# A fused multiply and GELU on one core: two DRAM stretches of 64 KB rows, two stores, and x opened by the heads of its rows

## The chip, the cores and the metric

The kernel runs on one core of a Trainium2 chip. The metric is the device time of one execution in microseconds; the figure given is the median of several runs. A profile of one execution shows when each engine worked and when each DMA packet moved.

## The reference

```python
batch, dim = 1024, 4096          # x and y: float32, normally distributed
z = x * y
out = (0.5 * z * (1 + np.tanh(np.sqrt(2 / np.pi) * (z + 0.044715 * z ** 3)))).astype(np.float32)
```

Every element stands by itself. The kernel reads two arrays of 16.78 MB and writes one, 50.33 MB in all.

## The kernel before

Since the operation is elementwise, the kernel treats each array as one flat run of 4,194,304 values and may give any part of it to any of the 128 partitions, as long as x, y and the output agree. On chip, `xs` holds 32,768 values in each partition, all of x at once; the product and the result are written over it in place. `ys` holds 20,440 values in each partition, so y does not fit whole: its later part reuses room that the first part has left.

The flat run is cut into three pieces (`PIECES`), by columns of `xs`: columns 0 to 1280, 1280 to 17664 and 17664 to 32768. In DRAM each piece is one stretch without holes; the helper `columns` gives partition p the p-th run of it. One load of a piece is therefore 128 rows, of 5,120, 65,536 and 60,416 bytes. The rows of a transfer are dealt out to 16 DMA engines, eight to each.

The order of the transfers is written out by hand.

- x's small piece goes out from SP's queue and x's 64 KB rows from ACT's queue; `_hoist` moves both to the front of the program, ahead of the opening barrier.
- SP then waits for the small piece of x, and issues y's piece with 64 KB rows and x's third piece.
- y's third piece goes into room that the first three multiplies free, so SP waits for three of them (`Y_FREE`); y's small piece waits for the fourth. They land in `ys` from 0 and from 15104.
- VectorE (DVE) multiplies in the order of `Y_LOADS`: four steps of 4096 columns of the middle piece, then seven of 2048 and one of 768 of the third, then 1280 of the small one (`STEPS`). Before each piece it waits for x and y to have landed. ScalarE (ACT) waits for each multiply and applies GELU in place.
- SP stores the pieces in the same order (`STORES`), each when its activations are done; the first also waits until y's third piece has landed. At the end SP waits for all stores.

All of SP's transfers, loads and stores, stand in one queue in order of issue; in the profile it is q1, and ACT's queue, with x's 64 KB rows, is q10.

Of the kernel before, what the change touches and what calls it, by code (L numbers as in the profile page):

```python
# [1 line left out]

# [4 lines left out]


F32 = mybir.dt.float32
GELU = mybir.ActivationFunctionType.Gelu_apprx_tanh  # L10

PIECES = [(0, 1280), (1280, 17664), (17664, 32768)]

Y_LOADS = [(1280, 17664, 4056), (17664, 32768, 0), (0, 1280, 15104)]

Y_FREE = [0, 3, 4]

STEPS = [[4096] * 4, [2048] * 7 + [768], [1280]]  # L20
STORES = [(1280, 17664), (17664, 32768), (0, 1280)]
Y_BUF = 20440


def _hoist(nc, issued):

    here = nc.cur_bb.bb.instructions
    first = nc.main_func.blocks[0].instructions
    for ins in issued:
        del here[next(k for k, i in enumerate(here) if i is ins or i.name == ins.name)]  # L30
    engine = issued[0].engine
    at = next(
        k
        for k, i in enumerate(first)
        if i.engine == engine and type(i).__name__ == "InstDrain"
    )
    first[at:at] = issued


@with_exitstack  # L40
def kernel(
    ctx: ExitStack,
    tc: tile.TileContext,
    x: bass.AP,
    y: bass.AP,
    out: bass.AP,
):
    nc = tc.nc
    P = nc.NUM_PARTITIONS

    def columns(t, a, b):

        flat = t.flatten_outer_dims().rearrange("r c -> (r c)")
        pa, pb = next(q for q in PIECES if q[0] <= a and b <= q[1])
        return flat[P * pa : P * pb].rearrange("(p c) -> p c", p=P)[:, a - pa : b - pa]


    tc.close()
    tc.compile()  # L59

    xs = nc.alloc_sbuf_tensor("xs", [P, PIECES[-1][1]], F32).ap()
    ys = nc.alloc_sbuf_tensor("ys", [P, Y_BUF], F32).ap()
    sem_x = [nc.alloc_semaphore(f"sem_x{i}") for i in range(len(PIECES))]
    sem_y = [nc.alloc_semaphore(f"sem_y{i}") for i in range(len(Y_LOADS))]
    sem_mul = nc.alloc_semaphore("sem_mul")
    sem_act = nc.alloc_semaphore("sem_act")
    sem_o = [nc.alloc_semaphore(f"sem_o{i}") for i in range(len(STORES))]

    def load_x(i, engine=nc.sync):
        a, b = PIECES[i]  # L70
        return engine.dma_start(out=xs[:, a:b], in_=columns(x, a, b)).then_inc(sem_x[i], 16)

    def load_y(i):
        a, b, r = Y_LOADS[i]
        return nc.sync.dma_start(
            out=ys[:, r : r + b - a], in_=columns(y, a, b)
        ).then_inc(sem_y[i], 16)

    _hoist(nc, [load_x(0).ins])
    _hoist(nc, [load_x(1, nc.scalar).ins])  # L80
    nc.sync.wait_ge(sem_x[0], 16)
    load_y(0)
    load_x(2)
    for i in range(1, len(Y_LOADS)):
        if Y_FREE[i]:
            nc.sync.wait_ge(sem_mul, Y_FREE[i])
        load_y(i)

    n = 0
    done = {}  # L90
    for i, (a, b, r) in enumerate(Y_LOADS):
        for j, (xa, xb) in enumerate(PIECES):
            if xa <= a < xb:
                nc.vector.wait_ge(sem_x[j], 16)
        nc.vector.wait_ge(sem_y[i], 16)  # L95
        c = a
        for w in STEPS[i]:
            nc.vector.tensor_mul(  # L98
                out=xs[:, c : c + w],
                in0=xs[:, c : c + w],  # L100
                in1=ys[:, r + c - a : r + c - a + w],
            ).then_inc(sem_mul, 1)
            n += 1
            done[c + w] = n
            nc.scalar.wait_ge(sem_mul, n)
            nc.scalar.activation(  # L106
                out=xs[:, c : c + w], in_=xs[:, c : c + w], func=GELU
            ).then_inc(sem_act, 1)
            c += w

    for i, (a, b) in enumerate(STORES):
        if i == 0:
            nc.sync.wait_ge(sem_y[-2], 16)
        nc.sync.wait_ge(sem_act, done[b])
        nc.sync.dma_start(out=columns(out, a, b), in_=xs[:, a:b]).then_inc(sem_o[i], 16)
    for i in range(len(STORES) - 1):
        nc.sync.wait_ge(sem_o[i], 16)
    nums = sorted(s.num for s in [*sem_x, *sem_y, *sem_o[:-1], sem_mul, sem_act])
    assert nums == list(range(nums[0], nums[-1] + 1))
    nc.sync.sem_clear(range(nums[0], nums[-1] + 1))  # L120
    nc.sync.wait_ge(sem_o[-1], 16).then_inc(sem_o[-1], -16)


# [1 line left out]
_INS = ['x', 'y']  # L125
_OUTS = [((1024, 4096), 'float32')]


# [23 lines left out]
```

## Time and profile before

| What | Value |
|---|---|
| Median of 3 runs (lowest, highest) | 119.83 us (119.79, 119.85) |
| Span of the profiled execution, first to last instruction | 118.52 us |
| DVE busy, 13 multiplies | 35.2 us |
| ACT busy, 13 activations and a table load | 31.0 us |
| DMA moved | 50.33 MB, mean 425 GB/s, 1296 packets |
| Landings: x's pieces | 13.55, 30.48, 60.41 us |
| Landings: y's pieces | 42.56, 78.25, 79.82 us |
| Landings: stores | 99.19, 116.98, 118.49 us |

The profiled execution has no time of its own beside its span; the median of the runs is 1.31 us longer than that span, since a run's time takes in what lies before the first and after the last instruction. A line such as L98 is a line of the kernel's file; DVE's multiplies carry L98, ACT's activations L106, y's loads L75, x's loads L71 and the stores L115 in the listing of the profile. "Landing" is the moment when all 16 DMA engines have reported a transfer to its semaphore.

### The profile page before, as it was taken

How to read it: one execution, taken by the hardware profiler on the slowest of the kernel's cores; microseconds unless marked ns; L12 is line 12 of the kernel's file. 1: busy time of each engine (PE TensorE's matmuls, PEld its weight loads, DVE VectorE, ACT ScalarE, POOL GpSimd, SP SyncE). 2: the span in 40 equal slices, each digit the busy share in tenths (PEclk: the TensorE clock that was granted, in tenths of full speed). 3: DMA queues.
4: the chain of work that ended last, by engine and by line, in shares of the span. 5: the costliest groups of instructions: out<-in, count | busy, mean ns of one | idle time of the engine just before them, and what ended most of it. 6: DMA issues, size and time to landing. Idle time of an engine off the chain costs nothing.

```text
span 118.5 us, 82 instructions
## 1 busy us (share of the span) xinstructions
DVE 35.2 (30%) x13; ACT 31.0 (26%) x14; POOL 0.2 (0%) x4
## 2 busy tenths in 40 slices
DVE  0000000000000069999920000059999940000000
ACT  4000000000000000977975000006998990000000
POOL 0000000000000000000000000000000000000000
DMA  9888899889988897797797797798899887977975
GB/s 492 382 382 382 354 575 487 354 354 398 664 354 354 354 652 326 326 652 326 326 632 347 326 632 347 326 575 354 354 531 531 354 354 326 652 326 326 652 326 221
DMA packets 1296, 50.33 MB, mean 425 GB/s; under 512 B 144, under 2 KB 144, under 8 KB 528
## 3 DMA queue, kind: packets, MB, share of 16 engines
q1 hardware_dynamic: 1152, 41.94, 82.2%
q10 hardware_dynamic: 144, 8.39, 16.5%
HBM read 33.55 MB, written 16.78 MB: 425 GB/s over the span
## 4 chain that ended last, share of the span: by engine, by line
DMA 55%; DVE 24%; ACT 3%; issue 1%; DVEq 0%
DMA ys<-in_y_dram 43%; DVE xs L98 24%; DMA xs<-in_x_dram 11%; ACT xs L106 3%; DVEq L95 0%
## 5 line engine op out<-in xcount | busy, mean ns | idle before, releaser
L98 DVE TENSOR_TENSOR xs<-xs,ys 128x2048 f32<-128x2048 f32 (+3 forms) x13 | 35.2, 2777 | 60.9 <-DMA ys<-in_y_dram 60.9
L106 ACT ACTIVATE xs<-xs 128x2048 f32<-128x2048 f32 (+3 forms) x13 | 29.7, 2301 | 65.1 <-DVE xs L98 65.1
L106 ACT ACT_TABLE_LOAD x1 | 1.3, 1283 | 1.6 <-PEq L59 1.6
L136 POOL MEMSET const-bfloat16-1.0<- 128x1 bf16 x1 | 0.1, 103 | 0.0
L136 POOL MEMSET const-uint8-127<- 128x1 uint8 x1 | 0.1, 102 | 0.0
L136 POOL MEMSET const-float32-0.0<- 128x1 f32 x1 | 0.1, 100 | 0.2 <-issue 0.2
L136 POOL MEMSET const-float32-1.0<- 128x1 f32 x1 | 0.1, 99 | 0.0
## 6 DMA issues: line engine op xcount, KB each, us to landing
xs<-in_x_dram SPq DMA_DIRECT2D x1, 7552.0 KB, 46.5
ys<-in_y_dram SPq DMA_DIRECT2D x1, 7552.0 KB, 22.5
out_dram<-xs SPq DMA_DIRECT2D x1, 7552.0 KB, 20.4
xs<-in_x_dram SPq DMA_DIRECT2D x1, 640.0 KB, 13.6
ys<-in_y_dram SPq DMA_DIRECT2D x1, 640.0 KB, 19.7
out_dram<-xs SPq DMA_DIRECT2D x1, 640.0 KB, 20.8
xs<-in_x_dram ACTq DMA_DIRECT2D x1, 30.4
ys<-in_y_dram SPq DMA_DIRECT2D x1, 29.0
```

Of the source, the lines that this page charges most:

```text
L98: nc.vector.tensor_mul(out=xs[:, c : c + w], in0=xs[:, c : c + w], in1=ys[:, r + c - a : r + c - a + w],).then_inc(sem_mul, 1)
L106: nc.scalar.activation(out=xs[:, c : c + w], in_=xs[:, c : c + w], func=GELU).then_inc(sem_act, 1)
L136: nc = _bacc.Bacc("TRN2", target_bir_lowering=False, num_devices=1)
```

## The change

The flat run is cut into two halves instead of three pieces (`HALVES`), so that partition p owns one run of 65,536 bytes in each half. A transfer that takes part of a half reads that part of each run: its rows then lie 65,536 bytes apart in DRAM.

- x's first half is loaded as two transfers: 5,120-byte heads of its rows from SP (`HEAD`), the remaining 60,416 bytes of each row from ACT. x's second half is one transfer of 64 KB rows.
- y's first half is one transfer of 64 KB rows; its second half is loaded as the first 48 KB of each row, then the last 16 KB, into `ys` from 0 and from 12288. They wait for three and for four multiplies, as the corresponding loads did.
- The multiplies go through the first half in four steps of 4096, then through the second in six steps of 2048 (48 KB rows) and steps of 2048, 1280 and 768 (16 KB rows).
- There are two stores of 64 KB rows instead of three. The first waits for four activations and for the first multiply of y's second half; the second for all 13 activations.

```diff
-PIECES = [(0, 1280), (1280, 17664), (17664, 32768)]
+HALF = 16384
+HALVES = [(0, HALF), (HALF, 2 * HALF)]
 
-Y_LOADS = [(1280, 17664, 4056), (17664, 32768, 0), (0, 1280, 15104)]
+HEAD = 1280
 
-Y_FREE = [0, 3, 4]
-
-STEPS = [[4096] * 4, [2048] * 7 + [768], [1280]]
-STORES = [(1280, 17664), (17664, 32768), (0, 1280)]
+Y_LOADS = [(0, 16384, 4056, 0), (16384, 28672, 0, 3), (28672, 32768, 12288, 4)]
+STEPS = [[4096] * 4, [2048] * 6, [2048, 1280, 768]]
...
-        pa, pb = next(q for q in PIECES if q[0] <= a and b <= q[1])
-        return flat[P * pa : P * pb].rearrange("(p c) -> p c", p=P)[:, a - pa : b - pa]
+        ha, hb = next(h for h in HALVES if h[0] <= a and b <= h[1])
+        return flat[P * ha : P * hb].rearrange("(p c) -> p c", p=P)[:, a - ha : b - ha]
...
-    _hoist(nc, [load_x(0).ins])
-    _hoist(nc, [load_x(1, nc.scalar).ins])
+    _hoist(nc, [load_x(0, HEAD, sem_x[0]).ins])
+    _hoist(nc, [load_x(HEAD, HALF, sem_x[1], nc.scalar).ins])
     nc.sync.wait_ge(sem_x[0], 16)
     load_y(0)
-    load_x(2)
+    load_x(*HALVES[1], sem_x[2])
     for i in range(1, len(Y_LOADS)):
-        if Y_FREE[i]:
-            nc.sync.wait_ge(sem_mul, Y_FREE[i])
+        nc.sync.wait_ge(sem_mul, Y_LOADS[i][3])
         load_y(i)
...
-    for i, (a, b) in enumerate(STORES):
-        if i == 0:
-            nc.sync.wait_ge(sem_y[-2], 16)
-        nc.sync.wait_ge(sem_act, done[b])
+    first = len(STEPS[0])
+    nc.sync.wait_ge(sem_act, first)
+    nc.sync.wait_ge(sem_mul, first + 1)
+    for i, done in enumerate((first, n)):
+        a, b = HALVES[i]
+        nc.sync.wait_ge(sem_act, done)
         nc.sync.dma_start(out=columns(out, a, b), in_=xs[:, a:b]).then_inc(sem_o[i], 16)
...
```

More of the change, by code (lines that the diff above doesn't have):

```diff
@@ L53, in columns @@
         flat = t.flatten_outer_dims().rearrange("r c -> (r c)")
-        pa, pb = next(q for q in PIECES if q[0] <= a and b <= q[1])
-        return flat[P * pa : P * pb].rearrange("(p c) -> p c", p=P)[:, a - pa : b - pa]
+        ha, hb = next(h for h in HALVES if h[0] <= a and b <= h[1])
+        return flat[P * ha : P * hb].rearrange("(p c) -> p c", p=P)[:, a - ha : b - ha]
     tc.close()
     tc.compile()
-    xs = nc.alloc_sbuf_tensor("xs", [P, PIECES[-1][1]], F32).ap()
+    xs = nc.alloc_sbuf_tensor("xs", [P, 2 * HALF], F32).ap()
     ys = nc.alloc_sbuf_tensor("ys", [P, Y_BUF], F32).ap()
-    sem_x = [nc.alloc_semaphore(f"sem_x{i}") for i in range(len(PIECES))]
+    sem_x = [nc.alloc_semaphore(f"sem_x{i}") for i in range(3)]
     sem_y = [nc.alloc_semaphore(f"sem_y{i}") for i in range(len(Y_LOADS))]
@@ L66, with load_x, load_y @@
     sem_act = nc.alloc_semaphore("sem_act")
[L67 to L75, printed above, removed]
+    sem_o = [nc.alloc_semaphore(f"sem_o{i}") for i in range(2)]
+    def load_x(a, b, sem, engine=nc.sync):
+        return engine.dma_start(out=xs[:, a:b], in_=columns(x, a, b)).then_inc(sem, 16)
+    def load_y(i, engine=nc.sync):
+        a, b, r, _ = Y_LOADS[i]
+        return engine.dma_start(
             out=ys[:, r : r + b - a], in_=columns(y, a, b)
         ).then_inc(sem_y[i], 16)
-    _hoist(nc, [load_x(0).ins])
-    _hoist(nc, [load_x(1, nc.scalar).ins])
+    _hoist(nc, [load_x(0, HEAD, sem_x[0]).ins])
+    _hoist(nc, [load_x(HEAD, HALF, sem_x[1], nc.scalar).ins])
     nc.sync.wait_ge(sem_x[0], 16)
     load_y(0)
-    load_x(2)
+    load_x(*HALVES[1], sem_x[2])
     for i in range(1, len(Y_LOADS)):
-        if Y_FREE[i]:
-            nc.sync.wait_ge(sem_mul, Y_FREE[i])
+        nc.sync.wait_ge(sem_mul, Y_LOADS[i][3])
         load_y(i)
     n = 0
[L90 to L94, printed above, removed]
+    for i, (a, b, r, _) in enumerate(Y_LOADS):
+        if i == 0:
+            nc.vector.wait_ge(sem_x[0], 16)
+            nc.vector.wait_ge(sem_x[1], 16)
+        if i == 1:
+            nc.vector.wait_ge(sem_x[2], 16)
         nc.vector.wait_ge(sem_y[i], 16)
@@ L103 @@
             n += 1
-            done[c + w] = n
             nc.scalar.wait_ge(sem_mul, n)
@@ L109 @@
             c += w
-    for i, (a, b) in enumerate(STORES):
-        if i == 0:
-            nc.sync.wait_ge(sem_y[-2], 16)
-        nc.sync.wait_ge(sem_act, done[b])
+    first = len(STEPS[0])
[4 more added lines that the diff above has]
+        nc.sync.wait_ge(sem_act, done)
         nc.sync.dma_start(out=columns(out, a, b), in_=xs[:, a:b]).then_inc(sem_o[i], 16)
-    for i in range(len(STORES) - 1):
-        nc.sync.wait_ge(sem_o[i], 16)
-    nums = sorted(s.num for s in [*sem_x, *sem_y, *sem_o[:-1], sem_mul, sem_act])
+    nc.sync.wait_ge(sem_o[0], 16)
+    nums = sorted(s.num for s in [*sem_x, *sem_y, sem_o[0], sem_mul, sem_act])
     assert nums == list(range(nums[0], nums[-1] + 1))
     nc.sync.sem_clear(range(nums[0], nums[-1] + 1))
-    nc.sync.wait_ge(sem_o[-1], 16).then_inc(sem_o[-1], -16)
+    nc.sync.wait_ge(sem_o[1], 16).then_inc(sem_o[1], -16)
 _INS = ['x', 'y']
```

## The prediction

> **What bounds the kernel now.** I read the page first: its busy shares and its list of DMA queues.
>
> ```profile
> span 118.5 us, 82 instructions
> DVE 35.2 (30%) x13; ACT 31.0 (26%) x14; POOL 0.2 (0%) x4
> ...
> q1 hardware_dynamic: 1152, 41.94, 82.2%
> q10 hardware_dynamic: 144, 8.39, 16.5%
> ```
>
> No engine that computes is busy for a third of the span, but the packets of the two DMA queues (q1 is SP's, q10 is ACT's) fill 82.2 + 16.5 = 98.7% of what 16 DMA engines could do in it. The chain that ended last seems to say otherwise:
>
> ```profile
> 0.00 13.55 DMA xs<-in_x_dram
> 13.57 28.99 DMA ys<-in_y_dram
> 42.66 13.11 DVE xs L98 x3
> 55.78 22.47 DMA ys<-in_y_dram
> 80.56 13.30 DVE xs L98 x6
> 93.88 3.80 ACT xs L106 x3
> ```
>
> It names 24% DVE, because it goes from issue to issue: y's second load is issued at 55.78, when three multiplies have freed its buffer. Whether that issue is late for the DMA engines it does not say. So I read the DMA by stages (columns: stretch, length, three engines' busy time, clock, DMA share, GB/s):
>
> ```profile
> 13.60:42.60 29.00, 0.00 (x0) 0.00 (x0) 0.00 (x0) 1.00 1.00 431
> 42.60:60.40 17.80, 17.43 (x4) 11.13 (x4) 0.00 (x0) 1.00 1.00 434
> 79.80:99.20 19.40, 16.32 (x9) 15.26 (x9) 0.00 (x0) 1.00 0.99 428
> ```
>
> The DMA share is 1 with and without the multiplies: the engines run at about 431 GB/s whatever DVE does. (A packet is booked where it starts, so short or badly cut stretches show more or less.)
>
> Last I took the trace's packet records (start, duration, bytes, queue) one by one and followed, from the last packet backwards, whichever ended 3 ns after it began. That gives the whole life of the DMA engine that ended last, 81 packets without a hole: 24 of each row size and 9 semaphore writes. In ns:
>
> ```
> row bytes   typical duration   step to the next packet
>  5,120        196                 193
> 60,416       2229                2226
> 65,536       2418                2414.5
>      4          9                   6
> last engine: first packet at 1312, last ends at 118123
> stretched packets: the first two of x (399, 342), the first two on ACT's queue (2549, 2620)
> ```
>
> The sum: 24 x 193 + 24 x 2226 + 24 x 2414.5 + 9 x 6 = 116.06 us. With the start at 1.31 and the stretched packets' excess (203 + 146 + 131 + 202 ns = 0.68) it is 118.05, against 118.12 measured; 0.07 is spread over small stretches. The final write lands 0.37 later, at 118.49, and the span closes at 118.52. The median of the runs, 119.83, lies 1.31 above that span, which I carry over. So what can move the time is: row counts, the first 13 us, a hole in the stream, and the last landing.
>
> **The change part by part.**
>
> *Rows.* Nine transfers of 8 rows per DMA engine become eight, with the same bytes. The steps above lie on a line (2033 ns for the 55,296 bytes between the two smaller sizes, 193 at 5,120), which puts a 49,152-byte row at 1812 and a 16,384-byte row at 607 ns. After, per engine: x's heads 8 x 193 = 1.54; the rest of x's first half 8 x 2226 = 17.81; y's first half, x's second half and two stores 32 x 2414.5 = 77.26; y's second half 8 x 1812 + 8 x 607 = 19.35; semaphores 8 x 6 = 0.05. Sum 116.02: a gain of 0.04 us, all on the path. No large gain is left in fewer rows: a row costs only about 5 ns beyond its bytes.
>
> *Row pitch.* The second half of x and of y and the second store, before in rows packed at 60,416 bytes, go to a 65,536-byte pitch in DRAM. Row of the trace: y's first load has that pitch now and takes 2418 to 2425 a packet, the 60,416-byte rows 2229 to 2246; both are 27.1 bytes per ns. Stores: the first (65,536) averages 2 to 18 ns over 2418 a packet after its first round, the second (60,416) 1 to 18 over 2229. I take nothing, with -0.05 to +0.1 for 8 store rows. The Trainium skill, "DMA: Bandwidth & Descriptors", section "Latency and other measured facts", speaks against such a layout: it has copies slow at row pitches of large powers of two, 207 GB/s at 512 KiB against 214 unimpaired (each DMA engine's eight rows here span that much). By that rule, as an estimate, 7 of 214 (3.3%) of the 25.2 MB that get this pitch, 58 us at 431 GB/s, would be 1.9 us; y's first load shows none of it.
>
> *Start.* x's heads were one packed 640 KB; now each lies at the front of its own 65,536-byte stretch. No row of the trace reads such heads, so bounds. The mean durations of x's five first rounds are 444, 222, 206, 203 and 198: only the first reads are slow. The last engine lost 0.68 in this stage; all of that gone would be -0.68. If instead each of its six later heads were stretched by as much as its second one is (146 ns), it would be +0.88. I take 0: the nearest row, ACT's load at the new pitch with its first packets 126 (mean), then 21 and 1 ns over 2418, says that scattered rows cost once and not on each row.
>
> *Issues, in SP's order; each only matters if the queue runs dry.* An issue brings its first packet about 0.84 later (the first store: 78.27 to 79.11); at the very start 1.01. y's first load waits for x's heads to land: now 13.55, and four ACT packets per engine that lie between the heads shorten by 188 each, so about 12.8. Meanwhile ACT's queue still has four of its eight packets per engine, 8.9 us of cover. x's second half is issued right behind it. y's 48 KB rows wait for multiply 3: y's first half lands 8 x 0.188 = 1.5 earlier (41.05), so the issue comes at 54.27; x's second half feeds the first engine until 59.5 as before, cover 4.4 after the 0.84. y's 16 KB rows wait for multiply 4 at 58.6 and are needed at 74.0.
>
> The first store has a new wait, the first multiply of y's second half. Behind it on SP stand only the second store and the closing waits. The 48 KB rows land at 78.25 - 8 x (2226 - 1812) ns = 74.94, the multiply ends 0.1 + 2.29 later at 77.33, so the first store packet can start at 78.19. The 16 KB rows hold the first engine until 78.89 and the last until 79.38: a cover of 0.70 and more. Today the cover is negative for the first engines (rows end at 78.90, store starts at 79.11; 0.10 us of hole on average: last semaphore writes end at 79.09, store packets start at 79.19 in the mean), while the last engine has none. Closing those holes helps engines that wait for the last one anyway; I count 0, at best -0.1.
>
> The second store now waits for all 13 activations. The same set of tile widths took from 78.35 to 97.68 = 19.33; started at 75.04 it ends at 94.4, and the first store feeds the engines until 98.5: cover 3.3. The third store's issue and wait disappear, hidden already.
>
> *End.* The last packets become 64 KB rows. From the last semaphore write's end to landing took 0.49 and 0.45 for the two large stores, 0.37 for the small last one: +0 to +0.12, and I take 0.05; less load at the end argues for the small side. The last store's 5 KB packets, some 4 ns over 196 each, take 0.03 away with them.
>
> Sum: -0.04 rows, 0 pitch, 0 start, 0 holes, +0.05 - 0.03 end = -0.02. The span stays at 118.5, the time at 119.83 - 0.02, say 119.80.
>
> **The rivals.** *Slower: heads scattered at 64 KB are slow reads.* Place: the first 2.6 us and the five rounds of x before ACT's packets come, then three more between them. For it: cold reads in this stage take up to 756 ns. Against it: ACT's and y's rows at this pitch are at full rate after the first. Price: 0.15 if each later head costs what round two costs on average (26 ns x 6), up to 0.88 as above; it decides from 40 ns per head. Middle of those that decide: +0.55, 120.35.
>
> *Faster: the stretched start relaxes.* The last engine's 0.68 is more than the mean engine's (305 ns of x's first load, 147 of ACT's: 0.45). If the new addresses spread the first reads so that the last engine loses only the mean, -0.23; with the first rounds of ACT's load free too, -0.38; with the other terms of the sum 119.43. Against it: the first-read delay of 0.25 on average looks like waiting for the first data, which no layout removes.
>
> *Slower by a hole:* if the new multiply wait delayed the first store by over 0.7 us, engines stand still for the rest. DVE's 2.29 for this tile is steady, so this is unlikely; price 0.3, 120.1.
>
> *That the gates matter* (y's first half lands 1.5 earlier, activations end 3.3 earlier, so a gain of 1.5 to 3): the full DMA shares speak against it, 118.3 or less, which I hold for almost excluded.
>
> **How the numbers follow.** No change 0.56; slow heads 0.20; relaxed start 0.19; a hole or large-row stores slower 0.04; gates 0.01. A measurement of this kernel can tell about 0.2%, 0.24 us, from no change. Hence faster 0.20, same 0.56, slower 0.24. The range takes the unknown end, pitch and closed holes (-0.15 to +0.2) and reaches to the larger part of the start's cases: 119.45 to 120.25. The forecast's own range is 119.62 to 120.02.
>
> **What would show it.** Right: DMA shares of 98 to 99%; 65,536-byte packets at 2418 throughout, 48 KB rows at about 1815; y's first half landing near 41.05, the 48 KB rows near 74.9, activations ending near 94.4, and a last landing still at 118.4 to 118.6; no hole between y's last rows and the first store. Wrong: packets of x's heads well over 196 after the second round, the first landing later than 12.8, store packets over 2430, or holes at 78 to 79 or 98.5.

## The result and the profile after

The changed kernel takes 120.19 us (median of 6 runs, 120.12 to 120.42) against 119.84 for the kernel before in the same comparison (6 runs, 119.76 to 119.91): ratio 1.003, interval 1.0017 to 1.0043. It is slower by 0.35 us where 119.80, no change, was forecast. The profiled execution took 120.17, its span is 118.84; before it was 118.52. So 0.32 of the 0.35 lies inside the span.

The page of the kernel after, busy shares and queues:

```profile
span 118.8 us, 79 instructions
DVE 35.2 (30%) x13; ACT 31.0 (26%) x14; POOL 0.2 (0%) x4
...
q1 hardware_dynamic: 1008, 42.60, 83.2%
q10 hardware_dynamic: 144, 7.73, 15.2%
```

The work is the same to a tenth of a microsecond, and the DMA packets still fill 98.4% of the span, with 144 packets fewer. The chain that ended last (start, length, what):

```profile
0.00 13.12 DMA xs<-in_x_dram
13.13 28.26 DMA ys<-in_y_dram
41.53 13.11 DVE xs L94 x3
54.65 20.63 DMA ys<-in_y_dram
75.37 15.52 DVE xs L94 x7
90.91 3.80 ACT xs L101 x3
```

Everything up to the stores does come earlier, as the change moves it: y's first half lands at 41.40, its 48 KB rows at 75.28, the activations end at 94.71. But each of these is 0.3 to 0.35 us later than the prediction's steps (41.05, 74.94, 94.4), and already the first piece, x's heads, lands at 13.12 where 12.8 was worked out. The later stages run at full rate (stretch, length, busy times, clock, DMA share, GB/s of the packets that begin in it):

```profile
1.00:1.80 0.80, 0.00 (x0) 0.23 (x1) 0.00 (x0) 1.00 0.83 179
13.10:41.40 28.30, 0.00 (x0) 0.00 (x0) 0.00 (x0) 1.00 1.01 436
80.20:99.50 19.30, 12.95 (x7) 13.05 (x8) 0.00 (x0) 1.00 1.00 435
```

The last two are at the full rate that the kernel before had. The first is the start, in which only 5 KB heads move and in which fewer bytes begin than in the kernel before, where it reads:

```profile
1.00:1.80 0.80, 0.00 (x0) 0.23 (x1) 0.00 (x0) 1.00 0.92 243
```

The packet records of the DMA engine that ended last say the same. Each row is a part of that engine's time in ns, from its first packet to the last landing:

```
                                          before    after
first packet starts                         1312     1515
its first packets of x, over 196 each       +349     +612   (after: the first takes 700, the eighth 304)
its packets on ACT's queue, over 2229/2418  +333     +196   (after: the fourth takes 2399)
rows and semaphores, by the steps         116060   116020
all else                                     +69      +26
last write ends                           118123   118369
lands                                     118491   118806
```

The differences are +203 + 263 - 137 - 40 - 43 = +246 ns up to the last write, and 69 more until it lands. So the three rows of the start make up the loss (+203 + 263 - 137 = +329 ns); the others nearly cancel. After 13 us this engine has no hole in either kernel, and no packet more than 17 ns over its nominal time.

### The profile page after: what moved, and what is told of

The parts are those of the page before. It is cut to its first block, busy times and chain, and to the rows that moved or that the text cites. A ratio compares the mean times of both kernels' runs of the same rounds, so it can differ in the third digit from the quotient of the medians.

```text
span 118.8 us, 79 instructions
## 1 busy us (share of the span) xinstructions
DVE 35.2 (30%) x13; ACT 31.0 (26%) x14; POOL 0.2 (0%) x4
## 4 chain that ended last, share of the span: by engine, by line
DMA 52%; DVE 24%; ACT 3%; issue 0%; DVEq 0%
DMA ys<-in_y_dram 41%; DVE xs L94 24%; DMA xs<-in_x_dram 11%; ACT xs L101 3%; DVEq L91 0%
```

## The experiments

"Time" is the median; the kernel before beside it was run on the same chip at the same time. "Heads' rounds" are the mean durations of x's first packets by rounds of 16 (one per DMA engine), over the nominal 196 ns. Where an edit reads x from other addresses, the output is not the reference's; the rows, their bytes and the work on the chip stay the same.

**The changed kernel once more, and the heads packed.** The first repeats the changed kernel as it is. The second kernel reads the heads from one stretch, `packed_head` in short.

```diff
-    _hoist(nc, [load_x(0, HEAD, sem_x[0]).ins])
+    packed = x.flatten_outer_dims().rearrange("r c -> (r c)")[: P * HEAD].rearrange("(p c) -> p c", p=P)
+    _hoist(nc, [nc.sync.dma_start(out=xs[:, 0:HEAD], in_=packed).then_inc(sem_x[0], 16).ins])
```

> The changed kernel as it stands, for a second profile and more times. If the late start is a property of the layout (theory 'heads': 5 KB heads lying 64 KB apart are slow first reads and set one DMA engine back for good), the time is 120.2 again, the first five rounds of x again average over 250 ns a packet on the first two rounds, and the last engine ends near 118.37. If it is chance of the one profiled execution (theory 'chance'), the stretched packets lie elsewhere and the last engine's end scatters by 0.3, though the median still is 120.2.

> The changed kernel, but the heads of x are read from one packed 640 KB stretch of x (other values than the reference wants, so the output is not the reference's in those columns; nothing else differs). Theory 'heads': the time falls back to 119.85 (119.75 to 119.95), the last engine's final write ends near 118.1. Rival 'rest' (what costs is ACT's load, rows of 60,416 bytes that begin 5,120 bytes into a 64 KB stretch, or the landing of two 64 KB stores): it stays at 120.2, with packets of x's heads faster but ACT's first packets as stretched as before.

The changed kernel again: 120.37 against 119.86 (1.0041, 1.0029 to 1.0053). Its packets are stretched elsewhere than in the first profile, heads' rounds +463, 150, 57 and then nothing, ACT's packets +2, 0, 0, 18 instead of +82, 0, 15, 104, and the last write ends at 118.63 instead of 118.37. So the size scatters by some 0.2 and single packets of one profile must not be read closely; that the start is slow does not scatter. Packed heads: 120.18 (1.0021, 1.0012 to 1.0029), last write at 118.39. That is less than the theory of the heads wanted: at most half of the loss is gone, and ACT's packets are stretched by 114, 40, 61 and 83.

**The same edit the other way round.** The kernel before, its small piece of x read as heads 64 KB apart.

```diff
-    _hoist(nc, [load_x(0).ins])
+    heads = x.flatten_outer_dims().rearrange("r c -> (r c)")[: P * 16384].rearrange("(p c) -> p c", p=P)[:, :1280]
+    _hoist(nc, [nc.sync.dma_start(out=xs[:, 0:1280], in_=heads).then_inc(sem_x[0], 16).ins])
```

> The kernel before, but its small piece of x is read as 5 KB heads 64 KB apart (other values than the reference wants in those columns). Theory 'heads': 120.1 to 120.2, that is +0.25 to +0.35 on the kernel before. Rival 'rest': 119.84, nothing changes.

120.26, +0.40 (1.0032, 1.0021 to 1.0044): the whole loss, with nothing else of the change in the kernel. Heads' rounds +455, 81, 33, 75, 35, together 679 where the kernel before has 305; ACT's packets after them are not stretched (17, 0, 0). By stages, the heads 64 KB apart:

```profile
1.00:1.80 0.80, 0.00 (x0) 0.23 (x1) 0.00 (x0) 1.00 0.91 122
1.80:2.60 0.80, 0.00 (x0) 0.80 (x1) 0.00 (x0) 1.00 0.86 282
2.60:5.00 2.40, 0.00 (x0) 0.25 (x1) 0.00 (x0) 1.00 1.12 473
```

The DMA share is near 1 all the time, but in the first stretch the packets that begin carry half of what they carry with packed heads (243): they are as large and last longer. At 1.8 to 2.6 none of ACT's large packets has begun; with packed heads 15 of the first 16 have, and are booked there whole (the kernel before, the same stretch):

```profile
1.80:2.60 0.80, 0.00 (x0) 0.80 (x1) 0.00 (x0) 1.00 3.65 1498
```

**No heads at all.** x's first half in one load from SP, y's first from ACT, both at the front, no wait between them.

```diff
-    _hoist(nc, [load_x(0, HEAD, sem_x[0]).ins])
-    _hoist(nc, [load_x(HEAD, HALF, sem_x[1], nc.scalar).ins])
-    nc.sync.wait_ge(sem_x[0], 16)
-    load_y(0)
-    load_x(*HALVES[1], sem_x[2])
+    _hoist(nc, [load_x(0, HALF, sem_x[0]).ins])
+    _hoist(nc, [load_y(0, nc.scalar).ins])
+    load_x(*HALVES[1], sem_x[1])
```

> The changed kernel without heads: x's first half goes as one transfer of 64 KB rows from SP and y's first half from ACT, both at the front, and SP no longer waits between them; x's second half follows. 8 rows and a transfer per engine less, -0.05. Theory 'heads': no small first reads, the only stretched packets are the first 64 KB rows (before: 126 ns in the mean), so 119.6 to 119.9. Rival 'rest', taken as any read at 64 KB pitch being slow at the start: no better than 120.2. A third possibility: without small packets the second queue's first packets come late and nothing is lost, since the engines have 64 KB rows to work on from 1.0 us.

120.12 (1.0024, 1.0012 to 1.0035), outside what any theory gave. The first 64 KB packets average 3030 ns instead of 2418, the later ones 2419: the start is paid in the first packet here, and small heads are not the only way to pay it: these rows follow one another without a gap.

**Is it the same address bits?** If each of the 16 engines takes eight rows that follow one another, the engines begin 8 x 64 KB apart and might all ask the same part of DRAM. (The profile holds no addresses, so which rows an engine takes is a supposition.) So: heads 68 KB apart in the kernel before; 59 KB rows first, 64 KB rows second; the version without heads with rows 68 KB apart; and packed heads taken from the far end of x, away from ACT's rows. The edits in this order:

```diff
+    heads = x.flatten_outer_dims().rearrange("r c -> (r c)")[: P * 17408].rearrange("(p c) -> p c", p=P)[:, :1280]
```

```diff
-PIECES = [(0, 1280), (1280, 17664), (17664, 32768)]
-Y_LOADS = [(1280, 17664, 4056), (17664, 32768, 0), (0, 1280, 15104)]
-STEPS = [[4096] * 4, [2048] * 7 + [768], [1280]]
-STORES = [(1280, 17664), (17664, 32768), (0, 1280)]
+PIECES = [(0, 1280), (1280, 16384), (16384, 32768)]
+Y_LOADS = [(1280, 16384, 5336), (16384, 32768, 0), (0, 1280, 16384)]
+STEPS = [[4096] * 3 + [2816], [2048] * 8, [1280]]
+STORES = [(1280, 16384), (16384, 32768), (0, 1280)]
```

```diff
-    _hoist(nc, [load_x(0, HALF, sem_x[0]).ins])
+    apart = x.flatten_outer_dims().rearrange("r c -> (r c)")[: P * 17408].rearrange("(p c) -> p c", p=P)[:, :HALF]
+    _hoist(nc, [nc.sync.dma_start(out=xs[:, 0:HALF], in_=apart).then_inc(sem_x[0], 16).ins])
```

```diff
-    packed = x.flatten_outer_dims().rearrange("r c -> (r c)")[: P * HEAD].rearrange("(p c) -> p c", p=P)
+    packed = x.flatten_outer_dims().rearrange("r c -> (r c)")[P * 2 * HALF - P * HEAD :].rearrange("(p c) -> p c", p=P)
```

> The kernel before, its small piece of x read as 5 KB heads 69,632 bytes apart (64 KB and 4 KB; other values than the reference wants in those columns). With heads 65,536 bytes apart it took 120.26 against 119.86. Theory 'same address bits' (16 DMA engines that begin 8 x 64 KB apart ask the same part of DRAM until they have drifted apart): 119.8 to 119.95, heads' first two rounds averaging as before (444, 222). Rival 'scattered' (every head opens a new place in DRAM whatever the distance): 120.2 to 120.3, first rounds near 651 and 277.

> The kernel before with its second and third piece exchanged in size: x's and y's first large loads have rows of 60,416 bytes packed, the second ones 64 KB; the small piece stays packed, the stores keep their order. Rows and bytes per engine are the same. Theory 'same address bits': ACT's first packets, which are stretched by 126 in the mean now, lose most of that since the engines begin 483,328 bytes apart: 119.65 to 119.8. Rival 'scattered' or 'only the heads matter': 119.86, no change.

> The version without heads, but the rows of x's first half are read 69,632 bytes apart (other values than the reference wants in the first half). At 65,536 bytes its first packets averaged 3030 ns against 2418 and nothing was stretched later. Theory 'same address bits': the first packets fall to about 2650 (the first round's 250 that even packed heads show), the time by up to 0.35, from 120.12 to 119.75 to 119.9. Rival 'cold start' (the first packets wait for something that has nothing to do with addresses): 3030 and 120.1 again.

> The changed kernel with the heads of x read from a packed 640 KB stretch at the very end of x, away from the rows that ACT's queue reads at the same time (other values than the reference wants in the heads). With the stretch at the front of x, inside those rows, it took 120.18. Theory 'collision' (heads and ACT's rows meet in the same region): 119.85 to 119.95. Rival 'ACT's rows too' (rows of 60,416 bytes in 64 KB stretches are stretched by themselves, and large last rows land 0.07 later): 120.15 to 120.2 again.

Heads 68 KB apart: 120.21 (1.004, 1.0025 to 1.0055), no better than 64. Without heads, 68 KB apart: 120.53 (1.0062, 1.005 to 1.0074), 0.4 worse than rows that follow without a gap. So the theory falls. Packed heads from afar: 120.17 (1.0031, 1.0019 to 1.0043), so that they lie among ACT's rows is not what costs. And 59 KB rows first: 121.86, +2.02. There ACT's first packets are stretched as before (+153 in the mean, against 126 and 146 in two profiles of the kernel before), and a hole opens that I had not worked out. The timeline and the DMA packets at 96.5 to 99.5 us of that kernel (40 slices; a packet is booked where it starts):

```profile
78.38 21.24 SPq L115 DMA_DIRECT2D out_dram<-xs  x3
96.20 3.07 ACT L106 ACTIVATE xs<-xs 128x2048 f32<-128x2048 f32 x2 [0.29 <-DVE xs L98]
```

```profile
DMA  0000000000000000000000000000000099990000
```

The first store, now of 59 KB rows, is through at 97.1 to 97.5. The second waits for the 2048 columns that ACT ends at 96.20 + 1.91 = 98.11, and its first packet starts at 98.97. The engine that ends last gets its first one at 99.13, at least 1.6 us after its last row of the first store. Most of the other 0.4 was there before the hole: the latest engine ends the first store at 97.53, where 98.71 as in the kernel before, less 8 x 0.1885 for the shorter rows, would be 97.20. Where that 0.33 arose stays open. The delay from issue to first packet, 0.85, is what the prediction used for its covers; this is what an uncovered one costs.

**A second profile of before, ACT's rows packed too, and a small last store.** In the second kernel the heads are packed, and ACT's rows of 60,416 bytes follow each other without a gap behind them. The third cuts the second store in two.

```diff
-    _hoist(nc, [load_x(0, HEAD, sem_x[0]).ins])
-    _hoist(nc, [load_x(HEAD, HALF, sem_x[1], nc.scalar).ins])
+    heads = flat[: P * HEAD].rearrange("(p c) -> p c", p=P)
+    rest = flat[P * HEAD : P * HALF].rearrange("(p c) -> p c", p=P)
+    _hoist(nc, [nc.sync.dma_start(out=xs[:, 0:HEAD], in_=heads).then_inc(sem_x[0], 16).ins])
+    _hoist(nc, [nc.scalar.dma_start(out=xs[:, HEAD:HALF], in_=rest).then_inc(sem_x[1], 16).ins])
```

```diff
-    for i, done in enumerate((first, n)):
-        a, b = HALVES[i]
+    PARTS = [HALVES[0], (HALF, 2 * HALF - HEAD), (2 * HALF - HEAD, 2 * HALF)]
+    for i, done in enumerate((first, n, n)):
+        a, b = PARTS[i]
```

> The kernel before as it stands, for a second profile of its start. Theory 'packed heads start faster': the first two rounds of x's heads again average near 444 and 222, ACT's first near 2540, the last engine's final write ends near 118.1, time 119.84. If the start scatters as much from execution to execution as the packed heads of the changed kernel did (first round 542 and 614), then one profile's packets cannot carry the comparison, and only the times can.

> The changed kernel, x's first half read as in the kernel before in pitch: heads packed, and ACT's rows of 60,416 bytes packed behind them (other values than the reference wants in the first half). With heads alone packed it took 120.18. Theory 'ACT's rows in 64 KB stretches cost the rest': 119.85 to 119.95. Rival 'rows of 60,416 bytes beside the heads stretch, packed or not' or 'the end': 120.15 to 120.2 again.

> The changed kernel with its second store cut in two, columns up to 31488 (59 KB of each row) and then the last 1280 (5 KB), so that the last packets are small as before. Theory 'landing': 64 KB last rows land 0.44 after the last write against 0.37, so 0.07 less, with 8 more rows and a semaphore 0.05 more: 120.15 to 120.37, no change within what can be told, and the lag in the profile back to 0.37. Rival 'the end costs the 0.3 that packed heads do not explain': 119.9 to 120.05.

Before again: 119.86 (1.0002, 0.9993 to 1.0011), heads' rounds +208, 28, 15: the fast start repeats. Start packed: 119.87 (1.0, 0.999 to 1.001). The loss is gone, although y's loads, x's second half and both stores are those of the changed kernel. This is the run that decides where the loss sits: in the two loads of x's first half and in nothing else. Its start:

```profile
1.00:1.80 0.80, 0.00 (x0) 0.23 (x1) 0.00 (x0) 1.00 0.96 288
```

Small last store: 120.35 (1.0049, 1.0036 to 1.0062), as the changed kernel, so the end is not it. The lag from the last write to its landing is 0.41 in it, with 5 KB rows, and 0.35 in the kernel with packed heads from afar, with 64 KB rows. These two are the exceptions, though: of the 20 profiles, the other seven that end with 64 KB rows have 0.40 to 0.45, and the other eleven that end with 5 or 10 KB rows 0.33 to 0.38. So the changed kernel does land some 0.07 later after its last write, as the term for large last rows had it. Since the lag is 0.41 with small last rows in the changed kernel, the size of the rows is not shown to be the reason.

**Distance, or an unbroken run?** A load whose rows follow without a gap might be set up faster. Here the kernel before reads its heads 5,376 bytes apart, or ACT's rows 65,792 bytes apart: 256 bytes of gap each. And ACT's load is issued behind the opening barrier, once as it is and once with pieces that start with 10,240-byte rows.

```diff
-    _hoist(nc, [load_x(0).ins])
+    heads = x.flatten_outer_dims().rearrange("r c -> (r c)")[: P * 1344].rearrange("(p c) -> p c", p=P)[:, :1280]
+    _hoist(nc, [nc.sync.dma_start(out=xs[:, 0:1280], in_=heads).then_inc(sem_x[0], 16).ins])
```

```diff
-    _hoist(nc, [load_x(1, nc.scalar).ins])
+    rows = x.flatten_outer_dims().rearrange("r c -> (r c)")[P * 1280 : P * (1280 + 16448)].rearrange("(p c) -> p c", p=P)[:, :16384]
+    _hoist(nc, [nc.scalar.dma_start(out=xs[:, 1280:17664], in_=rows).then_inc(sem_x[1], 16).ins])
```

```diff
-    _hoist(nc, [load_x(1, nc.scalar).ins])
+    load_x(1, nc.scalar)
```

```diff
-PIECES = [(0, 1280), (1280, 17664), (17664, 32768)]
+PIECES = [(0, 2560), (2560, 18944), (18944, 32768)]
...
-    _hoist(nc, [load_x(1, nc.scalar).ins])
+    load_x(1, nc.scalar)
```

> The kernel before, the heads of x read 5,376 bytes apart, with a gap of 256 bytes after each 5,120 (other values than the reference wants in those columns): nearly the same 640 KB of DRAM, but no unbroken run. Theory 'distance' (far-apart rows are slow first reads): 119.85, as before. Theory 'unbroken run' (a load whose rows do not follow without holes starts slower): 120.2 to 120.3, as with heads 64 KB apart, heads' rounds summing to 500 to 800 ns over nominal instead of 280 to 305.

> The kernel before, ACT's 64 KB rows read 65,792 bytes apart, a gap of 256 bytes after each (other values than the reference wants in those columns); heads packed. Theory 'distance': 119.85, since these rows lie as far apart in both. Theory 'unbroken run': 120.15 to 120.25, and the heads' first round slower (350 to 420 over nominal instead of 190 to 250) although their own load is untouched.

> The kernel before with ACT's load issued behind the opening barrier, about 1.6 us instead of 0.13. If the setting up of ACT's load delays the first packets of the heads, their first rounds shrink by 0.1 to 0.2 us, but the heads' 8 rows per engine run out near 2.8 us while ACT's first packets can come only near 3.8: a hole of about 1 us, time 120.6 to 121. If the two loads do not touch each other, the same hole with the heads unchanged.

> As late_act, with small pieces of 10,240-byte rows, so that SP's first load lasts until about 4.3 us and covers the late one. Nothing else changes but the sizes of the second piece's tail. If ACT's setting up delays the heads: 119.6 to 119.75, better than both kernels. If not: 119.8 to 119.9.

Heads with a 256-byte gap: 119.82 (0.9996, 0.9988 to 1.0005). ACT's rows with one: 119.87 (1.0002, 0.9993 to 1.0011). So a break of 256 bytes costs nothing that can be told. The start of the first of the two:

```profile
1.00:1.80 0.80, 0.00 (x0) 0.23 (x1) 0.00 (x0) 1.00 1.00 262
```

ACT's load late: 120.78 (1.0093, 1.0063 to 1.0123). Its heads' first round is +137, the least of the runs with 5 KB heads but one (+103), and ACT's first packets wait and take 2891. With 10 KB rows: 120.99 (1.0108, 1.0069 to 1.0148), not the gain I hoped for; the first round is +663 there, though these rows are packed. I have no explanation for that one.

**The step between engines, and the place of ACT's rows.** The heads 65,792 bytes apart in the kernel before, the whole of x's first half so in the changed kernel, and ACT's packed rows of the kernel before read from the front of x.

```diff
+    heads = x.flatten_outer_dims().rearrange("r c -> (r c)")[: P * 16448].rearrange("(p c) -> p c", p=P)[:, :1280]
```

```diff
+    rows = x.flatten_outer_dims().rearrange("r c -> (r c)")[: P * 16448].rearrange("(p c) -> p c", p=P)
+    _hoist(nc, [nc.sync.dma_start(out=xs[:, 0:HEAD], in_=rows[:, 0:HEAD]).then_inc(sem_x[0], 16).ins])
+    _hoist(nc, [nc.scalar.dma_start(out=xs[:, HEAD:HALF], in_=rows[:, HEAD:HALF]).then_inc(sem_x[1], 16).ins])
```

```diff
+    rows = x.flatten_outer_dims().rearrange("r c -> (r c)")[: P * 16384].rearrange("(p c) -> p c", p=P)
+    _hoist(nc, [nc.scalar.dma_start(out=xs[:, 1280:17664], in_=rows).then_inc(sem_x[1], 16).ins])
```

> The kernel before, the heads of x read 65,792 bytes apart, that is 64 KB and 256 bytes (other values than the reference wants in those columns). The engines' first addresses step by 526,336 bytes, 257 times 2 KB, where 64 KB gave 524,288 and 68 KB gave 557,056, 17 times 32 KB. Theory 'same address bits, below 32 KB': 119.85, heads' rounds summing to about 300 over nominal. Theory 'distance': 120.2 to 120.3, sum 650 to 780.

> The changed kernel, with the rows of x's first half (heads and ACT's part) read 65,792 bytes apart instead of 65,536 (other values than the reference wants in the first half). Theory 'same address bits, below 32 KB': 119.85 to 119.95 instead of 120.2 to 120.4. Theory 'distance': 120.2 to 120.4.

> The kernel before, ACT's packed 64 KB rows read from the very front of x, where the heads lie, instead of 640 KB further (other values than the reference wants in those columns). The heads stay packed. If packed heads beside ACT's 59 KB rows were slow (120.17) because of where ACT's rows begin: 120.1 to 120.2. If it was the 5 KB left out between these rows: 119.85.

Heads 65,792 apart: 120.23 (1.0035, 1.0023 to 1.0046); all of the first half so: 120.34 (1.0041, 1.0027 to 1.0055). They are as slow as at 65,536, so the exact step plays no part. ACT's rows from the front: 119.93 (1.0003, 0.9994 to 1.0013), so where they begin plays none. The start of the second of the three:

```profile
1.00:1.80 0.80, 0.00 (x0) 0.23 (x1) 0.00 (x0) 1.00 1.14 134
```

All kernels with 5 KB heads and ACT's load at the front, but the one with the hole, by the gaps that the first two loads leave in DRAM between one row and the next (difference of medians; GB/s in the stretch 1.0 to 1.8 us):

```
                            gap of heads  gap of ACT's rows   us      GB/s
before                                0           0            -      243
before again                          0           0         +0.02     269
start packed                          0           0         +0.03     288
near-packed heads                   256           0         +0.01     262
near-packed ACT rows                  0         256         +0.06     237
ACT's rows from the front             0           0         +0.06     269
packed heads, changed kernel          0        5120         +0.32     205
packed heads from afar                0        5120         +0.33     154
heads 64 KB apart                 60416           0         +0.40     122
heads 68 KB apart                 64512           0         +0.37     141
heads 65,792 apart                60672           0         +0.36     154
changed kernel                    60416        5120         +0.35     179
the same again                    60416        5120         +0.51     109
changed, 65,792 apart             60672        5376         +0.47     134
changed, small last store         60416        5120         +0.51     115
```

The six rows without a gap of over 256 bytes lie within 0.06 of before, the nine with one lie 0.32 to 0.51 above, and none stands between. The two effects hardly add up. In the pair without heads a gap costs too (no gap 120.12, a gap of 4 KB 120.53), but the one without a gap is itself 0.26 above the kernel before: a gap is not the only thing that makes a start slow. None of the kernels beats the kernel before by more than can be told; the best, 119.82, is equal to it.

## Why the prediction was wrong

*What held.* The bound: DMA shares at 1 behind the start, 435 to 436 GB/s. The row steps: 49,152-byte packets take 1815 (step 1812) and 16,384-byte ones 611 (step 607), as interpolated. The covers: no hole at 78 to 79 us, none at 98.5; SP's new wait for the first multiply costs nothing, since the store's first packets come behind y's last rows without a break. The gates come 1.2 to 3 us earlier and bring no time, so that rival fell. The pitch of the later loads and the stores costs nothing that can be told: start packed has all of it at 119.87. The 1.9 us that the prediction worked out as an estimate from the Trainium skill's row on large pitches ("DMA: Bandwidth & Descriptors", "Latency and other measured facts") are in no run here; that row measures copies whose rows, one for each partition, lie 512 KiB and more apart, and the rows here lie 64 KB apart. 4 KiB more between rows, which that row found to restore the rate at a pitch of 4 MiB, did not help the heads (120.21).

*What failed.* The step "Start ... I take 0". On the engine that ended last the start cost 0.33 us more than before; the prediction's sign for it, a first landing later than 12.8, came (13.12). The reason given for the 0 was the nearest row, ACT's first packets at the new pitch, with 126, 21 and 1 ns over nominal, read as "scattered rows cost once and not on each row". The reading of the shape was fair: heads 64 KB apart cost in the first two or three rounds (+455, 81, 33) and not in all eight. But the cost was taken as already paid, from a load that was unlike the heads in two ways: ACT's rows then had that pitch without a gap between them, and the engines had been reading for over a microsecond when they came (2.30 against 1.01 us), while the heads are the very first reads. That being first matters is likely and not tested alone; in the kernel without heads, 64 KB rows that come first took 612 over 2418 where ACT's took 126. Measured alone (heads 64 KB apart in the kernel before), the term is +0.40 instead of 0. It lay inside the prediction's own bound of -0.68 to +0.88, and is what the rival "slow heads" described, with the right place and near its price of 0.55, but not its condition, 40 ns and more on each of the six later heads: from the third round on they are 24 ns over in the mean.

*What no step had.* ACT's rows. That they leave out 5 KB each was counted as nothing but fewer bytes, and with packed heads this alone costs 0.32. Runs that change one part show that it is not their length (start packed), not where they begin (ACT's rows from the front) and not a gap as such (256 bytes); of what was varied, the gap of 5 KB is left. Since both causes lead to the same loss and do not add up, undoing only the heads looked like half an answer.

*The terms at the end.* They held. Later landing +0.05: 0.07 measured, and of that size over the other profiles, though its reason is open (small last store). Small last packets -0.03: the stretched packets outside the start fell by 0.04, as the stores of the kernel after take 2418 to 2419 throughout. The rows gave the -0.04 that was worked out. So the whole miss is the start. Two small readings were off without bearing on the sum: after its first round the first store of the kernel before averages 5 to 18 over 2418, and the second 1 to 6 over 2229.

*What stays open.* Why a gap of some KB between rows slows the first 0.8 us. In particular: why a gap in ACT's rows slows the packed heads, which move before any of ACT's packets is recorded. The table is a description found after the runs, which fits its 15 rows, not a mechanism. Between 256 bytes and 4 KB no gap was tried, and for the heads a wide gap always came with a wide spread of addresses (8 MB instead of 0.7), so that these two are told apart for ACT's rows only.

## What to carry to other kernels

In a kernel whose DMA engines never rest, as here, what is lost in the first microseconds is not made up later: in the kernels before and after, the engine that was last through x's first rows ended last, and its steps from then on went by the bytes. So cost the first transfers by themselves, from the first rounds of packets, and do not take a price for a cold first read from a load that started behind another. Here the first transfers should have rows that follow one another in DRAM, or nearly (256 bytes did no harm), while a pitch of 64 KB in the later ones cost nothing that can be told.

## What the hardware showed that I had not expected

A DMA engine that falls behind in the start stays behind by nearly the same amount to the end: in the changed kernel the engines' semaphore writes spread over 0.70 us after x's heads and 0.66 us at the last store. A hole brings them together: the kernel before has one for the early engines at 78.9 to 79.1, and its spread falls from 0.49 to 0.18 over the first store. It gains nothing by that, since the last engine does not wait. Where the engines then run closely in step their packets are a little longer (64 KB stores 2423 to 2436 on average after the first round, against 2418 to 2419 for the spread-out engines of the kernel after).
